# Expert outputs added through a second accumulator pair, spread over a column group; gates and scales fetched once for two experts

## The chip, the cores and the metric

The kernel runs on one core of a Trainium2 chip. Its engines run side by side and meet through semaphores: TensorE (PE; its weight loads are listed apart as PEld), VectorE (DVE), ScalarE (ACT), GpSimd (POOL) and SyncE (SP), which issues the weight transfers. Each engine takes its instructions in the order in which the program gives them. The metric is the device time of one execution in microseconds (us); the profile shows one execution, taken by the hardware profiler.

## The reference

Two decoder layers on 256 tokens of width 1024, in float32. Each layer has attention and a convolution that share an input and an output projection, and then a channel mixer: a dense SwiGLU in layer 0, routed experts in layer 1. The change touches the routed experts only. With `h` the normed tokens, they compute

```
logits = h @ router                       # 256 x 8
top_logit, top_e = top_k(logits, 2)       # two experts of each token
gate = softmax(top_logit)                 # one gate for each of the two
y_e = (silu(h_e @ wg[e]) * (h_e @ wu[e])) @ wd[e]     # h_e: the tokens that chose expert e
out = x + sum over the two experts of gate * y_e
```

with `wg`, `wu` of 1024 x 3584 and `wd` of 3584 x 1024 for each of eight experts.

## The kernel before

All weights stream from HBM through nine tiles of 1 MB (`raw`, line 165, issued by SP as a tile comes free). For float32 precision each matmul is made of three: a weight half tile is split by ACT into a rounded part `wh` (line 189) and by DVE into the rest `wl` (line 190), and `mm3` (lines 275 to 277) multiplies the high part by both and the low part by the high one. There are four pairs of `wh`/`wl` buffers, so splits run up to three half tiles ahead of PE.

The expert stage begins near 590 us and runs over the experts `e` (0 to 7), and in each over seven column groups `fc` of 512 hidden columns. `moe_in` (line 1308) makes the gate product in a bank of pool A and the up product in one of pool B (`pg`; eight steps `k` of three matmuls each), ACT applies SiLU, DVE multiplies (`sgm`, line 1329). `moe_out` (line 1347) adds the down product of the previous column group into `pd`, and in its middle `moe_tr` turns `sgm` by four transposes (`pt`, line 288) and splits it into `fh`, `fl`. The program is written out by hand in this order; nothing reorders it.

PSUM has eight banks: two of pool A, two of pool B, and two pairs of the pool `pacc` (`acc_bank`, line 97, a tile of two banks). `pd` of an expert takes one pair, so that consecutive experts alternate between the two pairs; the last expert takes the first bank of each. Small works are queued in the list `beside` and taken out one at a time behind the gate product's odd steps `k` (line 1322), four in a column group.

Which token sits in which of 128 slots of an expert is a one-hot matrix (`oh`, line 1229). Three things of an expert go through it:

- the tokens themselves, gathered by `gather` (line 1233) for a pair of experts in column groups 2 and 3 of the odd expert before;
- `turn_one_hot` (line 1378), behind the down product of column group 5: two transposes of the one-hot into a bank of pool A (`poh`), an ACT copy (`ohT`), then, in the same bank, two matmuls that fetch the expert's gate for each slot (`ge`, one column) with a DVE copy to `sgate`, and two that fetch the token scale of the next expert (`rs`, one column) with a DVE copy to `srs`;
- `combine` (line 1398): after an expert's last down product ACT and DVE make `yh` and `yl`, its output times the gates in two parts (`scaled`, lines 1394 and 1395). In column group 1 of the next expert four combines, for two column halves `n` and two token blocks `b`, multiply the turned one-hot by them into a bank of pool B (`pcomb`, lines 1402 and 1403) and DVE adds that to `xt` (line 1404). They stand in `beside`, so behind gate steps 1, 3, 5 and 7. The up product that follows needs a bank of the same pool B.

A last loop serves experts chosen by more than 128 tokens; it reads the gates and scales from the routing's own tiles.

Of the kernel before, what the change touches and what calls it, by code (L numbers as in the profile page):

```python
# [23 lines left out]
NB = 2  # L24
# [45 lines left out]
def trunk(ctx: ExitStack, tc: tile.TileContext, x, positions, attn_norm_g, ffn_norm_g, w_in, w_out,  # L70
# [28 lines left out]
    # ------------------------------------------------------------------ the stream of weights  # L99
# [49 lines left out]
    class Stream:  # L149
        """Weight tiles in the order of use: loads run RAW tiles ahead, the split into two  # L150
        float32r parts runs WB - 1 half tiles ahead."""
# [21 lines left out]
        def whole(self):  # L173
            """the next tile that is used as it is, and its number"""
            n = self.order[1].pop(0)
            return n, self.raws[n]
# [29 lines left out]
        def take_group(self, n):  # L206
            """n parts of one half tile each that are used more than once: no half tile beyond
            the buffers is split before their use"""
            return [self.take(WB - j) for j in range(n)]
# [9 lines left out]
    # ------------------------------------------------------------------ first loads  # L219
# [17 lines left out]
    # ------------------------------------------------------------------ constants  # L237
# [24 lines left out]
    # ------------------------------------------------------------------ helpers  # L262
    def rsqrt_mean(dst, ss, n):
        """dst = (ss / n + eps) ** -0.5"""
        w = ss.shape[-1]
        p = ss.shape[0]
        nc.vector.tensor_scalar(dst, ss, 1.0 / n, EPS, op0=ALU.mult, op1=ALU.add)
        nc.gpsimd.tensor_tensor(dst, dst, nhalf[:p, :w], op=ALU.pow)
# [15 lines left out]
    def transpose_split(src, hi, lo, bank):  # L284
        """src [128, 512] -> hi/lo [128, 4, 128]"""
        pt = bank("pt").rearrange("p (k t) -> p k t", k=4)
        for k in range(4):
            nc.tensor.transpose(pt[:, k], src[:, k * P:(k + 1) * P], ident)  # L288
        evac_split(hi, lo, pt)

    class Norm:
        """The transposed rms norm of xt, block by block, as hi/lo [128, 8, 256]; res: what is
        added to xt first"""
# [44 lines left out]
    def boundary(key, nrm, tails, heads, banks, **more):  # L338
        """the end of one part and the start of the next, with the norm between them; the order is
        that of the letters: o, a unit of the end (the last four those of the second token block);  # L340
        h, a unit of the start for the first block; z y x and a q u t, the norm of the two blocks;
        m, half a weight tile to split"""
        ops = dict(o=lambda: tails.pop(0)(), h=lambda: heads.pop(0)(), m=stream.more,
                   z=lambda: nrm.scale(0), y=lambda: nrm.mul(0), x=lambda: nrm.tr(0, banks),
                   a=lambda: nrm.add(1), q=lambda: nrm.square(1), u=lambda: nrm.mul(1), t=lambda: nrm.tr(1, banks),
                   **more)
        for c in BOUNDS[key]:
            ops[c]()

    # ------------------------------------------------------------------ rest of the setup  # L350
# [103 lines left out]
    def rope(sm, v, cs, sn):  # L454
        """v [n, heads, 64]; the first 16 of the last axis rotated in place"""
        n, h = v.shape[0], v.shape[1]
        t1 = sm.tile([P, HEADS, 16], F32, name="rope1", bufs=1)[:n, :h]
        t2 = sm.tile([P, HEADS, 16], F32, name="rope2", bufs=1)[:n, :h]
        csb = cs.rearrange("p a b -> p (a b)")[:, None, :].to_broadcast([n, h, 16])
        nc.vector.tensor_tensor(t1, v[:, :, :16], csb, op=ALU.mult)  # L460
        nc.vector.tensor_tensor(t2[:, :, :8], v[:, :, 8:16],
                                sn[:, 0][:, None, :].to_broadcast([n, h, 8]), op=ALU.mult)
        nc.vector.tensor_tensor(t2[:, :, 8:], v[:, :, :8],
                                sn[:, 1][:, None, :].to_broadcast([n, h, 8]), op=ALU.mult)
        nc.vector.tensor_tensor(v[:, :, :16], t1, t2, op=ALU.add)

    # ================================================================== layers
    for layer in range(DEPTH):
# [16 lines left out]
        # ---- queries, token-major  # L485
# [70 lines left out]
        # ---- inputs of the convolution, channel-major: two chunks of 128 channels at a time  # L556
# [28 lines left out]
        # causal depthwise conv, tap by tap beside other work: the first taps of a chunk on VectorE,  # L585
        # some on TensorE, the others multiplied on ScalarE and summed on GpSimd
# [20 lines left out]
        def tap_p(pair, j, first, last):  # L607
            """a tap of two chunks on TensorE, by diagonal matrices"""
# [32 lines left out]
        # ---- keys and values of the causal branches: token-major  # L641
# [41 lines left out]
        # ---- attention: the two causal branches, 512 score columns a step; the steps of both  # L683
        # token blocks form one pipeline
# [26 lines left out]
        # ---- inputs of the compressed branch and gates, channel-major  # L711
# [50 lines left out]
        # ---- compressed keys and values  # L762
# [74 lines left out]
        # ---- the steps of attention after the scores  # L837
# [79 lines left out]
        # ---- layer norm of the conv over channels and swish  # L917
# [52 lines left out]
        # ---- output projection  # L970
# [64 lines left out]
        # ---- channel mixer  # L1035
# [5 lines left out]
        # the scale of the tokens is left out where the experts apply it  # L1041
# [9 lines left out]
        def logits(b):  # L1051
            """the router's logits of a token block, channel-major"""
            bs = slice(b * P, (b + 1) * P)
            for k in range(DK):
                nc.tensor.matmul(pl[:16, bs], rt2[:, k], hT[:, k, bs], start=(k == 0), stop=False)
                nc.tensor.matmul(pl[:NE, bs], rt2[:, k, :NE], hTL[:, k, bs], start=False, stop=(k == DK - 1))
            nc.scalar.copy(lgT[:, bs], pl[:16, bs])
# [9 lines left out]
        if layer % 2 == 0:  # L1067
# [44 lines left out]
            def ffn_first():  # L1112
                """the first columns, token-major: the first token block starts before the second"""
# [70 lines left out]
        # ---- routed experts  # L1184
# [10 lines left out]
        # rank of each logit in its row; equal logits rank by index  # L1195
# [12 lines left out]
        # slot of each token within its expert: tokens before it that chose the same expert  # L1208
# [3 lines left out]
        ge = act.tile([P, NB, NE], F32, name="ge")  # L1212
# [20 lines left out]
        def gather(pair, banks):  # L1233
            """the tokens of a pair of experts, channel-major; in units of 256 channels and one part"""
# [23 lines left out]
        sgate = act.tile([P, NE], F32, name="sgate")  # L1258
        srs = act.tile([P, NE], F32, name="srs")
# [8 lines left out]
        def of_slots(dst, ps, e, src):  # L1268
            """a value of each token, for the tokens in the slots of an expert"""
            for b in range(NB):  # L1270
                nc.tensor.matmul(ps, ohs[e // 2].bitcast(F32)[:, b, e % 2], src[:, b:b + 1], start=(b == 0), stop=(b == NB - 1))
            nc.vector.tensor_copy(dst, ps)

        # experts chosen by more than 128 tokens: their number, indices, slots and gates
# [33 lines left out]
        def moe_in(e, fc, beside):  # L1308
# [4 lines left out]
            for bank in (bank_a, bank_b):  # L1313
                pg = bank("pg")
                for k in range(DK):
                    if first:
                        first.pop(0)()
                    if pgu and k == 2:
                        nc.scalar.activation(sg, pgu[0], AF.Silu, scale=srs[:, e:e + 1])
                    wh, wl = stream.take(2 if last and pgu else WB)  # L1320
                    mm3(pg, xg[:, k], xgL[:, k], wh, wl, k == 0, k == DK - 1)
                    if k % 2 and bank is bank_a and beside:
                        beside.pop(0)()
                if (e, fc) == (0, 0) and bank is bank_a:
                    of_slots(srs[:, 0:1], bank_b("psr")[:, :1], 0, rs)
                pgu.append(pg)
            for j in range(2 if last else 1):
                fs = slice(j * 256, (j + 1) * 256) if last else slice(0, 512)
                nc.vector.scalar_tensor_tensor(sg[:, fs], pgu[1][:, fs], srs[:, e:e + 1], sg[:, fs],
# [46 lines left out]
        ohTs, ys = {}, {}  # L1376

        def turn_one_hot(e):
            pt = bank_a("poh").rearrange("p (b t) -> p b t", b=4)
# [4 lines left out]
            of_slots(sgate[:, e:e + 1], pt[:, 2, :1], e, ge[:, :, e])  # L1384
            if e + 1 < NE:
                of_slots(srs[:, e + 1:e + 2], pt[:, 2, 1:2], e + 1, rs)

        def scaled(e, n):
            """the outputs of the expert times the gates, in two parts"""
# [4 lines left out]
            nc.scalar.activation(yh, pd, AF.Copy, scale=sgate[:, e:e + 1])  # L1394
            nc.vector.scalar_tensor_tensor(yl, pd, sgate[:, e:e + 1], yh.bitcast(F32),
                                           op0=ALU.mult, op1=ALU.subtract)

        def combine(e, n, b):
            ns = slice(n * 512, (n + 1) * 512)
            yh, yl = [y[:, ns] for y in ys[e]]  # L1400
            pc = bank_b("pcomb")
# [7 lines left out]
        beside = []  # L1409
        parts = [(n, b) for n in range(2) for b in range(NB)]  # L1410
        for e in range(NE):
            for fc in range(7):
                if fc == 1 and e:
                    beside += [lambda e=e, n=n, b=b: combine(e - 1, n, b) for n, b in parts]
# [3 lines left out]
                if fc == 2 and e % 2 == 1 and e + 1 < NE:  # L1418
                    beside += gather((e + 1) // 2, (bank_b, bank_b))
                if down_first(layer, NE - 1 - e, fc):  # L1420
# [10 lines left out]
                if fc == 5:  # L1431
                    turn_one_hot(e)
# [6 lines left out]
        # slots 128..255 of the experts that have them  # L1439
# [101 lines left out]
```

## Time and profile before

| | |
|---|---|
| median of three runs | 1623.56 us |
| the three runs | 1615.91, 1625.65, 1623.56 us |
| span of the profiled execution, first to last instruction | 1617.5 us |
| its own time, with what lies around the span | not recorded apart from the three runs |
| PE busy, whole span | 1546.0 us, 96% |
| DVE busy | 1342.1 us, 83% |
| ACT busy | 1093.4 us, 68% |
| DMA, mean rate | 268 GB/s over the span |
| TensorE clock granted, mean | 0.971 of full speed |

A matmul's record lasts longer than the distance to the next one, since matmuls overlap; how long a step takes is therefore read from the distance between starts. In the timeline an idle time of the engine before an instruction stands in brackets with what ended it. A clock of 0.50 is 1.2 GHz, of 1.00 it is 2.4 GHz.

### The profile page before, as it was taken

Reading aid. Unit: us, or ns where it says so; the run is one execution under the profiler, and the core shown is the slowest. Engines: PE = TensorE matmul, PEld = TensorE weight load, DVE = VectorE, ACT = ScalarE, POOL = GpSimd, SP = SyncE. Lnnn points to the kernel's source line nnn. Section 1 sums busy time; section 2 is a strip of 40 time slices with the busy share of each in tenths; the row PEclk is TensorE's granted clock in tenths of the full one; section 3 lists DMA queues with packets and bytes.
Section 4 is the critical chain, followed back from the end, with each engine's and each line's share of the span. In section 5 each row is a group of like instructions: output and inputs, shape, how many; then the busy total and the mean of one; then the engine's idle time right before and its main releaser. Section 6 shows DMA issues by size and latency. Waiting matters only on the chain.

```text
span 1617.5 us, 21390 instructions
## 1 busy us (share of the span) xinstructions
PE 1546.0 (96%) x7861; PEld 1294.0 (80%) x7861; DVE 1342.1 (83%) x1647; ACT 1093.4 (68%) x1430; POOL 126.0 (8%) x152
## 2 busy tenths in 40 slices
PE   6989999999997989999999999999999999999997
PEld 5977899999796768878877877887877877878785
DVE  7898655554789889989989989989989989998995
ACT  5765544444466568777877877777877777777774
POOL 2453000000155200000000000000000000000000
PEclk9978999999997999999999999999999999999998
DMA  9700585546632249999999998999999999998990
GB/s 307 223 27 1 187 304 182 183 167 198 158 105 79 79 151 373 378 323 335 362 336 337 371 337 314 359 349 338 371 339 330 338 353 329 367 369 314 362 364 27
DMA packets 197744, 433.75 MB, mean 268 GB/s; under 512 B 10346, under 2 KB 28978, under 8 KB 197636
## 3 DMA queue, kind: packets, MB, share of 16 engines
q1 hardware_dynamic: 196902, 432.02, 75.6%
q8 instruction: 63, 1.03, 0.3%
q0 software_dynamic: 288, 0.30, 0.1%
q14 instruction: 45, 0.37, 0.1%
q10 hardware_dynamic: 446, 0.03, 0.0%
HBM read 431.27 MB, written 1.05 MB: 267 GB/s over the span
## 4 chain that ended last, share of the span: by engine, by line
PE 77%; DVE 17%; ACT 3%; issue 2%; DMA 1%; POOL 0%; SPq 0%; DVEq 0%; ACTq 0%
PE pg L275 12%; PE pg L277 12%; PE pg L276 12%; PE pd L277 7%; PE pd L276 7%; PE pd L275 7%; DVE wl L190 5%; DVE cv L593 4%; PE pgu L275 3%; PE pgu L277 3%; PE pgu L276 3%; PE pt L288 2%; ACT wh L189 1%; PE pgx L1243 1%; DVE xt L1404 1%
## 5 line engine op out<-in xcount | busy, mean ns | idle before, releaser
L190 DVE TENSOR_TENSOR wl<-raw,wh 128x1024 fp32r<-128x1024 f32 x808 | 981.3, 1227 | 189.3 <-ACT wh L189 164.7
L189 ACT CAST wh<-raw 128x1024 fp32r<-128x1024 f32 x808 | 845.9, 1052 | 326.7 <-PE pg L277 126.4
L275 PE MATMUL pg<-wh,xgH 128*128 128x512 f32 x896 | 353.8, 395 | 6.5 <-DVE xt L1404 6.5
L277 PE MATMUL pg<-wh,xgL 128*128 128x512 f32 x896 | 353.5, 394 | 0.0
L276 PE MATMUL pg<-wl,xgH 128*128 128x512 f32 x896 | 352.5, 393 | 0.0
L275 PE MATMUL pd<-wh,fh 128*128 128x512 f32 x560 | 226.5, 404 | 0.1
L276 PE MATMUL pd<-wl,fh 128*128 128x512 f32 x560 | 222.2, 397 | 1.3 <-DVE wl L190 1.3
L277 PE MATMUL pd<-wh,fl 128*128 128x512 f32 x560 | 222.9, 398 | 0.0
L275 PEld LDWEIGHTS pg<-wh,xgH 128*128 128x128 f32 x896 | 170.3, 190 | 43.8 <-ACT wh L189 9.3
L277 PEld LDWEIGHTS pg<-wh,xgL 128*128 128x128 f32 x896 | 169.9, 190 | 36.5 <-DVE xgL L1247 0.5
L276 PEld LDWEIGHTS pg<-wl,xgH 128*128 128x128 f32 x896 | 170.5, 190 | 35.8 <-DVE wl L190 0.3
L276 PEld LDWEIGHTS pd<-wl,fh 128*128 128x128 f32 x560 | 105.8, 189 | 24.9 <-DVE wl L190 2.0
L277 PEld LDWEIGHTS pd<-wh,fl 128*128 128x128 f32 x560 | 105.6, 189 | 25.1 <-DVE fl L272 0.2
L275 PEld LDWEIGHTS pd<-wh,fh 128*128 128x128 f32 x560 | 105.9, 189 | 22.8 <-ACT fh L271 0.3
L275 PE MATMUL pgu<-hFH,wh 128*128 128x256 f32 x384 | 108.9, 284 | 0.8 <-DVE posT L452 0.8
L277 PE MATMUL pgu<-hFH,wl 128*128 128x256 f32 x384 | 108.7, 283 | 0.0
L276 PE MATMUL pgu<-hFL,wh 128*128 128x256 f32 x384 | 108.7, 283 | 0.0
L603 POOL TENSOR_TENSOR cvg<-cvg,tap 128x256 f32<-128x256 f32 x108 | 97.4, 929 | 75.4 <-ACT tap L602 71.9
L275 PEld LDWEIGHTS pgu<-hFH,wh 128*128 128x128 f32 x384 | 73.7, 192 | 1.1 <-PE pgk L1080 0.9
L276 PEld LDWEIGHTS pgu<-hFL,wh 128*128 128x128 f32 x384 | 73.7, 192 | 0.2
L277 PEld LDWEIGHTS pgu<-hFH,wl 128*128 128x128 f32 x384 | 73.7, 192 | 0.0
L593 DVE SCALAR_TENSOR_TENSOR cv<-hpad,cw,cv 128x256 f32<-128x256 f32 x124 | 72.2, 635 | 0.0
(371 smaller groups left out, 1655.1 us busy)
## 6 DMA issues: line engine op xcount, KB each, us to landing
raw<-in_moe_w_gate_dram SPq DMA_DIRECT2D x112, 1024.0 KB, 5.5
raw<-in_moe_w_up_dram SPq DMA_DIRECT2D x112, 1024.0 KB, 5.7
raw<-in_moe_w_down_dram SPq DMA_DIRECT2D x112, 1024.0 KB, 5.1
raw<-in_w_in_dram SPq DMA_DIRECT2D x18, 1024.0 KB, 9.5
raw<-in_ffn_w_gate_dram SPq DMA_DIRECT2D x14, 1024.0 KB, 7.9
raw<-in_ffn_w_up_dram SPq DMA_DIRECT2D x14, 1024.0 KB, 5.1
raw<-in_ffn_w_down_dram SPq DMA_DIRECT2D x14, 1024.0 KB, 4.9
raw<-in_w_out_dram SPq DMA_DIRECT2D x8, 1024.0 KB, 10.6
```

The lines of the kernel that those rows point to most:

```text
L189: nc.scalar.copy(h, r)
L190: nc.vector.tensor_tensor(lo, r, h.bitcast(F32), op=ALU.subtract)
L275: nc.tensor.matmul(dst, ah, bh, start=start, stop=False, skip_group_check=skip)
L276: nc.tensor.matmul(dst, ah, bl, start=False, stop=False, skip_group_check=skip)
L277: nc.tensor.matmul(dst, al, bh, start=False, stop=stop, skip_group_check=skip)
L288: nc.tensor.transpose(pt[:, k], src[:, k * P:(k + 1) * P], ident)
L593: nc.vector.scalar_tensor_tensor(cv[:, c], src, cw5[layer][:, c, j:j + 1], cv[:, c], op0=ALU.mult, op1=ALU.add)
L603: nc.gpsimd.tensor_tensor(cvg[:, c], cvg[:, c], tap, op=ALU.add)
L1243: nc.tensor.matmul(pgx, src[:, b, k * P:(k + 1) * P], ohs[pair][:, b].rearrange("p e s -> p (e s)"), start=(m == 0 and b == 0), stop=(m == ...
L1404: nc.vector.tensor_tensor(xt[:, b, ns], xt[:, b, ns], pc, op=ALU.add)
```

## The change

In column group 1 the four combines come from a list of their own, `spread`, taken out behind steps 1 and 5 of the gate product and of the up product. They write into an accumulator pair: `pcs[e]` is one `acc_bank` tile, and token block `b` uses its bank `b`. The last expert's combines keep pool B.

Token scales and gates of all experts sit in one tile `tv` (scale and eight gates for each token), for which DVE copies `rs` once in the routing. `slot_values` fetches all nine values for both experts of a pair by two units of two matmuls, in column group 4 of expert 0 and of each odd expert before the pair, and one DVE copy takes them to `sv`. Expert 0's first scale is still fetched alone at the beginning. `turn_one_hot` keeps its two transposes and the ACT copy, goes to `beside` in column group 5 (behind gate step 1), and uses pool B. Comments and docstrings are dropped elsewhere.

```
-        ge = act.tile([P, NB, NE], F32, name="ge")
+        tv = act.tile([P, NB, 1 + NE], F32, name="tv")
+        ge = tv[:, :, 1:]
+        nc.vector.tensor_copy(tv[:, :, 0], rs)
...
-        sgate = act.tile([P, NE], F32, name="sgate")
-        srs = act.tile([P, NE], F32, name="srs")
+        sv = act.tile([P, NE, 1 + NE], F32, name="sv")
+        srs = [sv[:, e, 0:1] for e in range(NE)]
+        sgate = [sv[:, e, 1 + e:2 + e] for e in range(NE)]
...
+        def slot_values(pair):
+            ps = {}
+            def unit(j):
+                if j == 0:
+                    ps["v"] = bank_b("psv")[:, :2 * (1 + NE)].rearrange("p (e n) -> p e n", e=2)
+                for b in range(NB):
+                    nc.tensor.matmul(ps["v"][:, j], ohs[pair].bitcast(F32)[:, b, j], tv[:, b],
+                                     start=(b == 0), stop=(b == NB - 1))
+                if j == 1:
+                    nc.vector.tensor_copy(sv[:, 2 * pair:2 * pair + 2], ps["v"])
+            return [lambda: unit(0), lambda: unit(1)]
...
                     if k % 2 and bank is bank_a and beside:
                         beside.pop(0)()
+                    if k % 4 == 1 and spread:
+                        spread.pop(0)()
...
         def turn_one_hot(e):
-            pt = bank_a("poh").rearrange("p (b t) -> p b t", b=4)
+            pt = bank_b("poh").rearrange("p (b t) -> p b t", b=4)
...
             nc.scalar.copy(ohTs[e], pt[:, :NB])
-            of_slots(sgate[:, e:e + 1], pt[:, 2, :1], e, ge[:, :, e])
-            if e + 1 < NE:
-                of_slots(srs[:, e + 1:e + 2], pt[:, 2, 1:2], e + 1, rs)
...
-            pc = bank_b("pcomb")
+            if e == NE - 1:
+                pc = bank_b("pcomb")
+            else:
+                if (n, b) == (0, 0):
+                    pcs[e] = acc_bank("pcomb")
+                pc = pcs[e][:, b]
...
                 if fc == 1 and e:
-                    beside += [lambda e=e, n=n, b=b: combine(e - 1, n, b) for n, b in parts]
+                    spread += [lambda e=e, n=n, b=b: combine(e - 1, n, b) for n, b in parts]
...
+                if fc == 4 and (e == 0 or e % 2 == 1 and e + 1 < NE):
+                    beside += slot_values((e + 1) // 2)
+                if fc == 5:
+                    beside += [lambda e=e: turn_one_hot(e)]
...
-                if fc == 5:
-                    turn_one_hot(e)
```

## Rows read from the trace of the kernel before

**Rows 1.** Busy time by stretch: us, PE, PEld, DVE, ACT, POOL, clock, DMA share, GB/s

```profile
720.00:845.00 125.00, 122.87 (x558) 100.19 (x557) 112.18 (x113) 95.01 (x105) 0.00 (x0) 0.99 0.93 337
...
902.80:919.70 16.90, 16.90 (x78) 13.85 (x76) 15.70 (x15) 13.55 (x15) 0.00 (x0) 1.00 1.01 367
```

**Rows 2.** Waits from 720 us on: who waited for whom, us, times, longest

```profile
ACT wh L189 <- PE pg L277: 110.1, 254, 3.0
...
PE pg L275 <- DVE xt L1404: 6.5, 7, 0.9
...
PE pd L276 <- DVE wl L190: 1.3, 2, 0.8
```

**Rows 3.** Timeline of PE at expert 1's turned one-hot: start, us, what

```profile
813.18 0.40 PE L277 MATMUL pd<-wh,fl 128*128 128x512 f32 x1
...
814.25 0.61 PE L1271 MATMUL poh<-ge,oh 128*128 128x1 f32 x4 [0.46 <-ACT ohT L1383]
815.18 0.60 PE L1271 MATMUL poh<-rs,oh 128*128 128x1 f32 x4 [0.32 <-DVE sgate L1272]
815.64 0.48 PE L275 MATMUL pg<-wh,xgH 128*128 128x512 f32 x1
...
816.19 0.63 PE L277 MATMUL pg<-wh,xgL 128*128 128x512 f32 x1
816.62 0.63 PE L275 MATMUL pg<-wh,xgH 128*128 128x512 f32 x1
```

**Rows 4.** Timeline of PE around four transposes inside a down product

```profile
809.93 0.40 PE L277 MATMUL pd<-wh,fl 128*128 128x512 f32 x1
...
810.52 0.48 PE L275 MATMUL pd<-wh,fh 128*128 128x512 f32 x1
```

**Rows 5.** Stretches of 3.41 us after a turned one-hot (two) and after a combine

```profile
816.17:819.58 3.41, 3.41 (x9) 2.64 (x8) 1.31 (x2) 1.04 (x1) 0.00 (x0) 0.50 0.78 229
...
687.00:690.41 3.41, 3.41 (x17) 2.78 (x16) 2.13 (x2) 1.78 (x2) 0.00 (x0) 1.00 0.68 209
...
730.06:733.47 3.41, 3.41 (x15) 2.85 (x16) 3.38 (x4) 1.74 (x3) 0.00 (x0) 1.00 0.84 294
```

**Rows 6.** Timeline of PE at the combines in column group 1 of expert 1

```profile
722.81 0.39 PE L275 MATMUL pg<-wh,xgH 128*128 128x512 f32 x1
...
725.82 0.39 PE L277 MATMUL pg<-wh,xgL 128*128 128x512 f32 x1
726.59 0.47 PE L1402 MATMUL pcomb<-yh,ohT 128*128 128x512 f32 x1 [0.39 <-DVE xt L1404]
...
728.74 0.40 PE L1403 MATMUL pcomb<-yl,ohT 128*128 128x512 f32 x1
730.06 0.47 PE L275 MATMUL pg<-wh,xgH 128*128 128x512 f32 x1 [0.92 <-DVE xt L1404]
```

**Rows 7.** Timeline of PE at the combines of expert 2

```profile
853.42 0.40 PE L275 MATMUL pg<-wh,xgH 128*128 128x512 f32 x1
...
856.70 0.47 PE L1402 MATMUL pcomb<-yh,ohT 128*128 128x512 f32 x1
```

**Rows 8.** Timeline of DVE in column group 1 of expert 1

```profile
725.76 0.68 DVE L1404 TENSOR_TENSOR xt<-xt,pcomb 128x512 f32<-128x512 f32 x1
726.36 1.22 DVE L190 TENSOR_TENSOR wl<-raw,wh 128x1024 fp32r<-128x1024 f32 x1
...
736.67 0.74 DVE L1329 SCALAR_TENSOR_TENSOR sgm<-pg,srs,sgm 128x512 f32<-128x512 f32 x1
```

**Rows 9.** Timeline of ACT: scaled outputs of expert 0 and of expert 7

```profile
722.46 0.69 ACT L1394 ACTIVATE yh<-pd,sgate 128x512 fp32r<-128x512 f32 x1 [0.92 <-DVE yl L1395]
...
1606.08 1.38 ACT L1394 ACTIVATE yh<-pd,sgate 128x512 fp32r<-128x512 f32 x2 [5.73 <-PE pd L277]
```

**Rows 10.** The page's DMA issues: count, KB each, us to landing

```profile
raw<-in_moe_w_gate_dram SPq DMA_DIRECT2D x112, 1024.0 KB, 5.5
```

**Rows 11.** Timeline of DVE in the routing

```profile
577.84 0.16 DVE L1214 TENSOR_REDUCE mx<-lg 128x2 f32<-128x16 f32 x1
```

More of the change, by code (lines that the diff above doesn't have):

```diff
@@ L1266, in gate_values, with slot_scale @@
             nc.vector.tensor_tensor(ge, ge, gs[:, :, None].to_broadcast([P, NB, NE]), op=ALU.mult)
-        def of_slots(dst, ps, e, src):
+        def slot_scale():
+            ps = bank_b("psr")[:, :1]
             for b in range(NB):
-                nc.tensor.matmul(ps, ohs[e // 2].bitcast(F32)[:, b, e % 2], src[:, b:b + 1], start=(b == 0), stop=(b == NB - 1))
-            nc.vector.tensor_copy(dst, ps)
+                nc.tensor.matmul(ps, ohs[0].bitcast(F32)[:, b, 0], rs[:, b:b + 1], start=(b == 0), stop=(b == NB - 1))
+            nc.vector.tensor_copy(srs[0], ps)
+        def slot_values(pair):
[9 more added lines that the diff above has]
+            return [lambda: unit(0), lambda: unit(1)]
         ov = act.tile([P, NE], F32, name="ov")
@@ L1318, in moe_in @@
                     if pgu and k == 2:
-                        nc.scalar.activation(sg, pgu[0], AF.Silu, scale=srs[:, e:e + 1])
+                        nc.scalar.activation(sg, pgu[0], AF.Silu, scale=srs[e])
                     wh, wl = stream.take(2 if last and pgu else WB)
@@ L1323, in moe_in @@
                         beside.pop(0)()
+                    if k % 4 == 1 and spread:
+                        spread.pop(0)()
                 if (e, fc) == (0, 0) and bank is bank_a:
-                    of_slots(srs[:, 0:1], bank_b("psr")[:, :1], 0, rs)
+                    slot_scale()
                 pgu.append(pg)
@@ L1328, in moe_in @@
                 fs = slice(j * 256, (j + 1) * 256) if last else slice(0, 512)
-                nc.vector.scalar_tensor_tensor(sg[:, fs], pgu[1][:, fs], srs[:, e:e + 1], sg[:, fs],
+                nc.vector.scalar_tensor_tensor(sg[:, fs], pgu[1][:, fs], srs[e], sg[:, fs],
                                                op0=ALU.mult, op1=ALU.mult)
@@ L1374, in moe_out @@
                     scaled(e, n)
-        ohTs, ys = {}, {}
+        ohTs, ys, pcs = {}, {}, {}
         def turn_one_hot(e):
-            pt = bank_a("poh").rearrange("p (b t) -> p b t", b=4)
+            pt = bank_b("poh").rearrange("p (b t) -> p b t", b=4)
             for b in range(NB):
@@ L1393, in scaled @@
             pd = pds[e][n] if e == NE - 1 else pds[e][:, n]
-            nc.scalar.activation(yh, pd, AF.Copy, scale=sgate[:, e:e + 1])
-            nc.vector.scalar_tensor_tensor(yl, pd, sgate[:, e:e + 1], yh.bitcast(F32),
+            nc.scalar.activation(yh, pd, AF.Copy, scale=sgate[e])
+            nc.vector.scalar_tensor_tensor(yl, pd, sgate[e], yh.bitcast(F32),
                                            op0=ALU.mult, op1=ALU.subtract)
@@ L1408, in trunk @@
         prev = None
-        beside = []
+        beside, spread = [], []
         parts = [(n, b) for n in range(2) for b in range(NB)]
```

## The prediction

> **What bounds the kernel now.** I read the busy time by stretch first, then the waits, then the timelines of single engines at the places that the change touches. Over a stretch of 125 us in the expert stage PE is busy 122.87 us and DVE 112.18 us; in an undisturbed column group PE fills all of the 16.90 us and DVE 15.70 us [rows 1]. The waits say the same from the other side: ACT waited 254 times, 110.1 us in all, for PE to free a buffer before it could split the next weights, while PE waited for a split of the down weights only twice, 1.3 us [rows 2]. So PE sets the pace here, and a stop of PE is paid in full unless another engine runs into PE's pace. Transfers are covered: a 1 MB tile lands 5.5 us after its issue [rows 10], a column group takes six of them in 16.90 us, 2.8 us each, and nine buffers therefore give some 25 us.
>
> One unit recurs below. From 722.81 to 725.82 us PE started 13 further matmuls [rows 6], so two neighbours stand 0.23 us apart at full clock.
>
> **The turned one-hot and the fetches.** Now each expert has a stop behind column group 5. From the last down matmul to the first gate matmul pass 815.64 - 813.18 = 2.46 us [rows 3], 2.23 us more than 0.23. Inside it PE waits for ACT's copy out of the bank, fetches gates, waits for the DVE copy, fetches scales. Experts 0 to 6 have this; expert 7 has no second fetch, 815.18 - 814.25 = 0.93 us less, so 1.30 us. Sum: 7 x 2.23 + 1.30 = 16.9 us.
>
> Afterwards two transposes stay for each expert. Four of them lengthen a distance from 0.23 to 0.59 us [rows 4], so two cost 0.18 us, eight times 1.4 us. A fetch unit is four short records again (two token blocks, two passes), and four such take 815.64 - 815.18 = 0.46 us [rows 3]. No row shows nine columns instead of one. Below, 0.46 us holds, since the records are as many; above, four full matmuls of 512 columns would take 4 x 0.23 = 0.92 us. Nine is near one, so I take 0.46, eight units, 3.7 us (up to 7.4). The part gains 16.9 - 1.4 - 3.7 = 11.8 us (8.1 at the other end).
>
> The ACT copy and the one DVE copy of a pair lie beside PE's next gate steps, because the up product that follows takes the other bank of pool B. If that cover failed, PE would wait 0.46 us for ACT as now [rows 3], 3.7 us in eight experts. The ACT copy waits for two transposes, and the casts queue behind it; DVE waits for these casts, and PE for DVE only after the three half tiles of lead, 18 x 0.23 = 4.1 us. I cost the wait at nothing. No DMA moves.
>
> **The clock.** After expert 1's one-hot the granted clock is 0.50 (1.2 GHz) for 3.41 us, with 9 matmuls, where a stretch after a combine has 15 at 1.00 [rows 5]. Two neighbours then stand 816.62 - 816.19 = 0.43 us apart [rows 3], so eight distances lose 0.20 us each, 1.6 us. Five of the eight experts show such a stretch right behind the one-hot (1, 2, 4, 5, 6); expert 0 does not [rows 5], nor do 3 and 7. Before each one PE had done little but short records for about 2.4 us. The stop of 1.09 us at a combine (below) is followed by full clock [rows 5], in all seven experts that have one. As the change leaves no stop much longer than that one, I take all five as gone: 8.0 us (bounds 0 and 8.0).
>
> **The combines.** In expert 1 the third combine begins 0.77 us behind its neighbour, and the up product 730.06 - 728.74 = 1.32 us behind the fourth, both waiting for a DVE add that must empty a bank of pool B [rows 6]. That loses 0.54 and 1.09 us. Experts 3 and 5 are alike; in 2, 4, 6 and 7, which build no new one-hots there, the third combine is hardly late (853.42 + 14 x 0.23 = 856.64 against 856.70 us [rows 7]) and the up product waits as long: seven such waits [rows 2]. Sum: 3 x 1.63 + 4 x 1.1 = 9.3 us.
>
> With the pair, the up product shares no bank with the combines, and that wait goes. What is late next is the second combine. The pair is one tile, and a pair seems to be held by one engine at a time: ACT's second `yh` of expert 0 waited 0.92 us for DVE's first `yl`, though they read different banks of one `pd` pair, while expert 7, whose `pd` are two tiles, runs both `yh` in 1.38 us without a break [rows 9]. Then the second combine, now behind gate step 5, waits for the first add. Its turn would be 722.81 + 12 x 0.23 = 725.57 us; the add ends at 725.76 + 0.68 = 726.44 [rows 8] and PE follows at 726.59, as the third combine does now [rows 6]: 1.02 us lost. In the even experts and in 7 it is 853.42 + 2.76 = 856.18 against 856.70 [rows 7], 0.52 us. The third comes 14 distances later, at 729.8 us; by then DVE has done two splits and the second add (726.36 + 2 x 1.2 + 0.68 = 729.4), so it does not wait, nor does the fourth. Behind the waiting combine are queued only the gate matmuls, priced with it. The product `sgm` is wanted 48 distances after the second combine, at 737.6 us; DVE, without a pause from 726.36 us on, ends it near 737.0 (now 736.67 + 0.74 [rows 8]). New stops: 3 x 1.02 + 4 x 0.52 = 5.1 us. Gain 9.3 - 5.1 = 4.2 us (7.4 at the other end, see the first rival).
>
> **The routing.** The copy of `rs` stands on DVE ahead of the reduction whose like took 0.16 us [rows 11], on the way to the first one-hots, with PE idle: 0.2 us lost (0 to 0.2).
>
> **Sum.** 11.8 + 8.0 + 4.2 - 0.2 = 23.8 us. On the profiled span that is 1617.5 to 1593.7. That execution's own time is not recorded beyond its span; the median, 1623.56, lies 6.1 us above it and one run, 1615.91, below it, so runs differ by some 10 us, which six half-clock stretches more or fewer would make (an estimate at 1.6 us each). I subtract from the median: 1599.8 us, as 1599.5.
>
> **First rival: no wait inside the pair.** If the program keeps engines apart by bank and not by tile, the second combine runs at 725.57 us. Then `sgm`, near 737.0, is late for its transposes at 725.57 + 48 x 0.23 = 736.6, some 0.6 us with the latency of 0.15, in experts 1, 3 and 5. The gain becomes 3 x 1.0 + 4 x 1.1 = 7.4 instead of 4.2: 1596.6 us. Against it stand the waits of `yh` [rows 9]. The Trainium skill speaks for it: its page "PSUM — Partial Sum Buffer" (section "PSUM bank collisions raise a hardware error") says that two engines may not touch one bank's quadrant at once and that accesses to different banks run clean. By that rule alone the time is 1596.6 us; the rows show a wait that it does not ask for. Chance 0.20.
>
> **Second rival: the drops of the clock stay**, caught by the stops and fetches that remain. Three of eight one-hots without a drop [rows 5] show that the stop alone does not decide. Gain 15.8 us: 1607.8. Chance 0.15.
>
> **Third rival, slower: the clock falls at the spread interruptions.** Eight turned one-hots, eight fetch units and 28 combines stand singly between gate and up matmuls. If each drew a half-clock stretch, 44 x 1.6 = 70 us would be added to the forecast: 1670 us. From 15 drops on (23.8 / 1.6) the kernel is slower than before, from 25 by over 1%. Against it: 28 combines are there already and none is followed by one [rows 5]. The Trainium skill knows such a case: "TensorE: Matmul & The Clock Gate", section "A second HAM failure mode: psum-queue depth-cycling", reports a kernel in which small idle times between groups of matmuls on changing PSUM banks made the clock go back and forth. The trace does not bear it out so far. Chance 0.08.
>
> **Fourth: the fetches and copies cost as much as they save**, PE waiting for ACT or DVE in column groups 4 and 5, where DVE has little room (15.70 of 16.90 us [rows 1]). Without the 11.8 us: 1611.6. Chance 0.07.
>
> **Numbers.** The forecast has 0.50. Its own range is 1595 to 1604 (3.7 us for dearer fetches, some 3 us if the median run had two drops more). Taking in the first and second rival and most of the fourth gives 1590 to 1611. A measurement can tell about 1% from no change, 16 us: faster means below 1607.3, slower above 1639.8. Faster: 0.50 + 0.20 + half of the second rival, 0.77. Slower: most of the third, 0.06. Same: the rest, 0.17.
>
> **What would show it.** Right: no `poh` fetch between column groups 5 and 6 and a gate matmul 0.23 us behind the last down matmul; no stretch at 0.50 in the expert stage before the last products; the up product of column group 1 no longer waiting for `xt`, and the second `pcomb` waiting 1.0 or 0.5 us for it. First rival: no such wait, and `pt` waiting for `sgm` in experts 1, 3 and 5. Wrong: half-clock stretches behind combines or fetches, PE waiting for `wl` or `wh`, or an expert's length falling by less than 1 us.

## The result and the profile after

The changed kernel takes 1595.55 us, the median of 4 runs (1593.36 to 1597.49), against 1624.29 us of the kernel before beside it (4 runs, 1615.91 to 1625.65): a ratio of 0.983, with a 95% interval of 0.981 to 0.986. 1599.5 us was forecast, with a range of 1590 to 1611. All medians of this document leave out one execution, of a kernel further below, which took 5051.78 us.

The profiled execution of after took 1595.13 us, close to its median. Its span is 1593.3 us, 24.2 us less than before's; 23.8 were forecast. The head of its page, with the clock in 40 slices:

```profile
span 1593.3 us, 21310 instructions
...
PE 1534.5 (96%) x7833; PEld 1289.9 (81%) x7833; DVE 1337.6 (84%) x1637; ACT 1093.3 (69%) x1430; POOL 122.1 (8%) x152
...
PEclk9978999999997789999999999999999999999999
```

From the sixteenth slice on (597 us), where the experts run, every slice shows the top digit. The same by stretches of after: the layers ahead with the experts' beginning, the expert stage, 125 us of it, then 3.41 us behind expert 0's turned one-hot and 3.41 us around the second combine (PE, PEld, DVE, ACT, POOL busy, clock, DMA share, GB/s):

```profile
0.00:588.00 588.00, 542.94 (x3349) 482.33 (x3350) 418.44 (x731) 315.26 (x596) 122.10 (x152) 0.92 0.47 153
...
588.40:1588.30 999.90, 991.16 (x4485) 807.31 (x4483) 918.77 (x907) 777.73 (x834) 0.00 (x0) 1.00 0.94 344
...
720.00:845.00 125.00, 124.17 (x572) 101.85 (x571) 114.89 (x117) 97.33 (x109) 0.00 (x0) 1.00 0.97 351
...
672.57:675.98 3.41, 3.41 (x18) 2.82 (x17) 2.76 (x3) 2.74 (x4) 0.00 (x0) 1.00 1.03 377
728.80:732.21 3.41, 3.41 (x16) 2.77 (x15) 3.41 (x5) 2.10 (x3) 0.00 (x0) 1.00 0.92 330
```

Where before PE was busy for 122.87 of 125 us [rows 1], it is now for 124.17 us, and it issues 572 matmuls there instead of 558. The stretch behind the one-hot holds 18 matmuls at full clock, against 9 at half clock before [rows 5].

The timeline of PE in after: expert 0's first scale, which is still fetched alone (`psr`, one column), a fetch unit, a turned one-hot, and the second combine in experts 1 and 2 (start, us, what; in brackets the idle time before and what ended it):

```profile
595.22 0.50 PE L1276 MATMUL psr<-rs,oh 128*128 128x1 f32 x4
595.58 0.47 PE L275 MATMUL pg<-wh,xgH 128*128 128x512 f32 x1
...
654.26 0.39 PE L277 MATMUL pg<-wh,xgL 128*128 128x512 f32 x1
654.50 0.51 PE L1287 MATMUL psv<-tv,oh 128*128 128x9 f32 x4
654.86 0.49 PE L275 MATMUL pg<-wh,xgH 128*128 128x512 f32 x1
655.18 0.40 PE L276 MATMUL pg<-wl,xgH 128*128 128x512 f32 x1
...
672.20 0.40 PE L277 MATMUL pg<-wh,xgL 128*128 128x512 f32 x1
672.43 0.38 PE L1403 MATMUL poh<-ident,oh 128*128 128x128 f32 x2
672.57 0.47 PE L275 MATMUL pg<-wh,xgH 128*128 128x512 f32 x1
672.89 0.39 PE L276 MATMUL pg<-wl,xgH 128*128 128x512 f32 x1
...
726.77 0.39 PE L277 MATMUL pg<-wh,xgL 128*128 128x512 f32 x1
727.95 0.50 PE L1426 MATMUL pcomb<-yh,ohT 128*128 128x512 f32 x1 [0.79 <-DVE xt L1428]
...
853.93 0.39 PE L277 MATMUL pg<-wh,xgL 128*128 128x512 f32 x1
854.59 0.50 PE L1426 MATMUL pcomb<-yh,ohT 128*128 128x512 f32 x1 [0.26 <-DVE xt L1428]
```

The fetch and the transposes stand between gate matmuls without a wait. What they cost is the distance that they add. A fetch unit adds 0.36 us, and the distance behind it is 0.32 instead of 0.23: 0.45 us in all, where 0.46 was taken. That 0.46 us was read from a fetch of one column behind a wait; `psr`, with no wait ahead of it, takes 595.58 - 595.22 = 0.36 us, as the nine columns do. Two transposes add 0.14 + 0.09 = 0.23 us, where 0.18 was taken. The second combine is late as forecast, by 727.95 - 726.77 - 0.23 = 0.95 us in expert 1 and by 0.43 us in expert 2.

The waits of after from 715 us on (in all, times, longest), to be read beside [rows 2]:

```profile
ACT wh L189 <- PE pg L277: 88.6, 235, 1.7
...
PE pcomb L1426 <- DVE xt L1428: 3.9, 8, 0.8
...
PE pd L276 <- DVE wl L190: 1.3, 2, 0.8
```

The wait of the up product for `xt` (6.5 us in 7 places before) is gone; the wait of the second combine has come in its place, in seven experts. (The eighth place, 0.42 us, is in the last expert, whose combines stay in pool B.) ACT still waits for PE as before: PE sets the pace.

### The profile page after: what moved, and what is told of

Its sections match the earlier page's. It is cut to its first block, busy times and chain, and to the rows that moved or that the text cites. A ratio compares the mean times of both kernels' runs of the same rounds, so it can differ in the third digit from the quotient of the medians.

```text
span 1593.3 us, 21310 instructions
## 1 busy us (share of the span) xinstructions
PE 1534.5 (96%) x7833; PEld 1289.9 (81%) x7833; DVE 1337.6 (84%) x1637; ACT 1093.3 (69%) x1430; POOL 122.1 (8%) x152
## 4 chain that ended last, share of the span: by engine, by line
PE 80%; DVE 14%; ACT 3%; issue 2%; DMA 1%; POOL 0%; SPq 0%; DVEq 0%; ACTq 0%
PE pg L275 12%; PE pg L277 12%; PE pg L276 12%; PE pd L277 8%; PE pd L276 8%; PE pd L275 7%; DVE cv L593 4%; DVE wl L190 4%; PE pgu L275 3%; PE pgu L277 3%; PE pgu L276 3%; PE pt L288 2%; ACT wh L189 1%; PE pgx L1246 1%; DVE nm L704 1%
## 5 line engine op out<-in xcount | busy, mean ns | idle before, releaser
L603 POOL TENSOR_TENSOR cvg<-cvg,tap 128x256 f32<-128x256 f32 x108 | 93.5, 891 | 80.1 <-ACT tap L602 76.3
```

What stands on the lines that cost most here:

```text
L603: nc.gpsimd.tensor_tensor(cvg[:, c], cvg[:, c], tap, op=ALU.add)
```

## The experiments

The theory behind the forecast was on record before these runs, in three parts: stops of PE are paid in full; a long one is paid a second time in half clock; and the second combine waits because the pair is one tile. The rivals were those of the prediction. Besides the time, the length of an expert is compared, from the first `yh` of the expert before to its own first `yh`, in one profiled execution each. Experts 3 and 4 stand for the odd ones (which build the next one-hots) and the even ones:

| us | time (median) | expert 3 | expert 4 |
|---|---|---|---|
| before | 1622 to 1624 | 129.03 | 126.19 (half clock) |
| combines alone | 1616.57 | 128.31 | 123.87 |
| fetches alone | 1602.27 | 127.85 | 122.45 |
| after | 1595.55, 1596.09 | 127.13 | 121.75 |
| one-hot in its old place | 1597.17 | 127.19 | 121.80 |
| old place and one fetch | 1603.40 | 128.23 | 122.73 |
| two tiles | 1592.18 | 126.34 | 121.19 |

**The combines alone.** The kernel before, with this part of the change only:

```
+                    if k % 4 == 1 and spread:
+                        spread.pop(0)()
...
-            pc = bank_b("pcomb")
+                if (n, b) == (0, 0):
+                    pcs[e] = acc_bank("pcomb")
+                pc = pcs[e][:, b]
...
-                    beside += [... combine(e - 1, n, b) ...]
+                    spread += [... combine(e - 1, n, b) ...]
```

> The kernel before with the combine part alone (spread list and accumulator pair); the turned one-hot and its fetches stay behind column group 5. My theory, that the two parts are separate terms: the stop of 2.2 us at each turned one-hot stays and with it half-clock stretches right behind four to six of the eight; the up product's wait of 1.09 us goes and the second combine waits 1.02 us (experts 1, 3, 5) or 0.52 us. The distance from one expert's first yh to the next falls by 0.6 us, seven times, so 4 us less than before, about 1620. Rival: the clock falls at the one-hot because of what the combines did earlier in the expert; then no stretch at 0.50 stands in the expert stage, and the time falls by 4 + 8 = 12 us, about 1612.

Measured 1616.57 us (6 runs, 1612.02 to 1618.38) against 1622.13, ratio 0.995 [0.994, 0.997]. Stretches of 3.41 us right behind the one-hots of experts 0 to 6 in this kernel (columns as above):

```profile
694.44:697.85 3.41, 3.41 (x9) 2.68 (x9) 1.50 (x2) 1.14 (x2) 0.00 (x0) 0.50 0.80 258
824.14:827.55 3.41, 3.41 (x9) 2.67 (x8) 1.69 (x2) 1.04 (x1) 0.00 (x0) 0.50 0.78 237
949.80:953.21 3.41, 3.41 (x17) 2.80 (x16) 1.95 (x3) 2.23 (x3) 0.00 (x0) 1.00 0.69 245
1078.10:1081.50 3.40, 3.40 (x17) 2.81 (x16) 1.98 (x3) 2.21 (x3) 0.00 (x0) 1.00 1.00 349
1201.90:1205.30 3.40, 3.40 (x16) 2.82 (x15) 1.98 (x3) 2.14 (x3) 0.00 (x0) 1.00 0.72 231
1329.32:1332.73 3.41, 3.41 (x10) 2.65 (x10) 1.29 (x2) 0.70 (x1) 0.00 (x0) 0.50 0.73 231
1455.61:1459.02 3.41, 3.41 (x9) 2.65 (x9) 1.66 (x2) 1.04 (x1) 0.00 (x0) 0.50 0.75 232
```

Half clock follows the one-hots of experts 0, 1, 5 and 6 here; before it was 1, 2, 4, 5 and 6. So the one-hot's stop brings it without the old combines too, though not every time. Expert 3, at full clock in both, is 0.72 us shorter, expert 1, at half clock in both, 0.68 us (0.61 forecast for odd experts). The time fell by more than 4 us; which half-clock stretches a run has differs, so this part's 4 to 5 us is read from the experts' lengths.

**The fetches and the turned one-hot alone.** After, with the combines as they were:

```
-                    pcs[e] = acc_bank("pcomb")
-                pc = pcs[e][:, b]
+            pc = bank_b("pcomb")
...
-                    spread += [... combine(e - 1, n, b) ...]
+                    beside += [... combine(e - 1, n, b) ...]
```

> The kernel after with the combines as before (behind gate steps 1, 3, 5, 7, in pool B); only the fetches and the turned one-hot are changed. My theory: the stops behind column group 5 go (11.8 us) and all half-clock stretches with them (8.0 us), less 0.2 us in the routing; the combines keep 7 waits of 1.09 us and three of 0.54 us. About 19.6 us less than before, 1604. Rival: the stops at the combines also feed the drops of the clock, so that stretches at 0.50 remain behind some experts' combines or fetches: 11.6 us less, 1612.6.

Measured 1602.27 us (1597.48 to 1604.10), ratio 0.987 [0.985, 0.989]: 19.9 us less than before beside it, 19.6 expected. The expert stage of this kernel and two of its waits between 700 and 1590 us, each view in a fence of its own:

```profile
592.20:1599.10 1006.90, 992.37 (x4486) 807.05 (x4485) 921.95 (x907) 779.76 (x834) 0.00 (x0) 1.00 0.94 341
```

```profile
PE pg L275 <- DVE xt L1423: 6.4, 7, 0.9
...
PE pcomb L1421 <- DVE xt L1423: 1.1, 3, 0.4
```

The clock is full throughout, and the up product's wait is the old one. All the clock's gain behind the one-hots therefore lies in this part, and the rival by which the half clock stays falls.

**The turned one-hot in its old place.** After, with only the fetches away from it:

```
-            pt = bank_b("poh")...
+            pt = bank_a("poh")...
...
-                if fc == 5:
-                    beside += [lambda e=e: turn_one_hot(e)]
...
+                if fc == 5:
+                    turn_one_hot(e)
```

> The kernel after, with the two transposes and the ACT copy of the one-hot moved back to their old place behind the down product of column group 5, in pool A; the fetches stay out of it. My theory: the stop came from the two fetches that waited in the same bank for ACT and DVE, not from the place; the gate product that follows takes the other bank of pool A, so there is no stop and no half-clock stretch, and the time is that of the kernel after within 1.5 us. Rival: the place itself, between down and gate product, makes PE wait (0.5 us or more for ACT, eight times) or lets the clock fall: 4 to 12 us more than the kernel after.

Measured 1597.17 us (1595.86 to 1599.47), ratio 0.985 [0.983, 0.987]. PE in this kernel, between the last down matmul and the first gate matmul:

```profile
688.73 0.40 PE L277 MATMUL pd<-wh,fl 128*128 128x512 f32 x1
688.97 0.38 PE L1403 MATMUL poh<-ident,oh 128*128 128x128 f32 x2
689.10 0.47 PE L275 MATMUL pg<-wh,xgH 128*128 128x512 f32 x1
```

PE does not stop: the gate product goes to the other bank of pool A. The stop came from the fetches in the one-hot's bank, not from the place of the transposes; moving them gives nothing measurable.

**One fetch again.** The kernel of the last experiment, with one gate fetch again in the one-hot's bank and a DVE copy behind it. The fetched value goes to a tile that nothing reads; the rest is computed as in after.

```
             nc.scalar.copy(ohTs[e], pt[:, :NB])
+            for b in range(NB):
+                nc.tensor.matmul(pt[:, 2, :1], ohs[e // 2]..., ge[:, b, e:e + 1], ...)
+            nc.vector.tensor_copy(sagain[:, e:e + 1], pt[:, 2, :1])
```

> The kernel with the transposes of the one-hot in their old place behind column group 5, and one fetch of the gates put back there in the same bank, with its DVE copy to a tile that nothing reads; the scales are not fetched there. That is about half of the stop of before: PE waits for ACT's copy, fetches, and goes on, 1.3 us in place of 2.2. My theory: it costs the stop alone, eight times 1.1 us more than without, 9 us, about 1605, and the clock stays at full speed as it did at expert 7 of the kernel before, whose stop was 1.3 us. Rival: half the stop is enough for the clock to fall behind several one-hots: 1.6 us more for each stretch, 1610 or more.

Measured 1603.40 us (1601.77 to 1605.65), ratio 0.987 [0.985, 0.990]. PE behind column group 5 of expert 0 in this kernel, and then its expert stage:

```profile
689.49 0.39 PE L277 MATMUL pd<-wh,fl 128*128 128x512 f32 x1
689.71 0.38 PE L1405 MATMUL poh<-ident,oh 128*128 128x128 f32 x2
690.56 0.61 PE L1409 MATMUL poh<-tv,oh 128*128 128x1 f32 x4 [0.46 <-ACT ohT L1407]
691.02 0.48 PE L275 MATMUL pg<-wh,xgH 128*128 128x512 f32 x1
```

```profile
590.10:1600.40 1010.30, 995.85 (x4517) 811.63 (x4515) 920.50 (x915) 777.34 (x834) 0.00 (x0) 1.00 0.94 340
```

The stop is back with 691.02 - 689.49 - 0.23 = 1.30 us, and an expert is 0.93 to 1.04 us longer (experts 4 and 3) than in the last experiment, where 1.1 was expected; the medians differ by 6.2 us, less than the 9 expected. The clock stays full. The eight stops of 1.3 us are paid once. The one of 2.23 us [rows 3], which experts 0 to 6 have, was paid twice in five of the seven before, and in four of the seven with the combines alone; each count is from one profiled execution.

**Two tiles for the combines.** After, with a tile of its own for each token block:

```
-                if (n, b) == (0, 0):
-                    pcs[e] = acc_bank("pcomb")
-                pc = pcs[e][:, b]
+                if n == 0:
+                    pcs[e, b] = acc_bank("pcomb")[:, 0]
+                pc = pcs[e, b]
```

> The kernel after, with the two token blocks of a combine in two accumulator tiles (the first bank of each) in place of two banks of one tile. My theory, that the program keeps engines apart by tile: the second combine no longer waits for xt (now 0.95 and 0.43 us of PE in the seven experts, 4.6 us in all); in experts 1, 3 and 5 the four transposes pt then wait some 0.5 us for sgm, as DVE has no slack there; 2 to 4 us less than the kernel after, about 1592.5. Rival 1: the wait is not the tile's but DVE's or the semaphore order's; the second combine still waits 0.4 to 1.0 us and the time is that of the kernel after. Rival 2: DVE gives all of it back, in waits for wl or sgm of the same sum: time as after within 1 us, but no wait for xt.

Measured 1591.25 us (four executions, 1590.68 to 1593.24; 1591.77 with the one of 5051.78), ratio 0.981 [0.979, 0.983]. The one left out was the profiled one, so the waits are read from the same kernel once more:

> The kernel with two accumulator tiles for the two token blocks once more, for a profile at the usual clock. Its runs gave 1591.8 us, some 4 us less than the kernel after. My theory, that the program keeps engines apart by tile: no pcomb waits for xt in the seven experts (4.6 us now), and pt waits about 0.5 us for sgm in experts 1, 3 and 5. Rival 1: the wait for xt is still there and the 4 us come from fewer half-clock stretches ahead of the expert stage. Rival 2: no wait for xt, but PE waits for wl instead, in sum less than 1 us better.

Measured 1592.18 us (1589.90 to 1593.38), ratio 0.980 [0.978, 0.982]. PE at the second combine of expert 1 in this kernel, and one of its waits from 700 us on:

```profile
729.19 0.39 PE L277 MATMUL pg<-wh,xgL 128*128 128x512 f32 x1
729.42 0.39 PE L1426 MATMUL pcomb<-yh,ohT 128*128 128x512 f32 x1
```

```profile
PEld pt L288 <- DVE sgm L1351: 1.3, 3, 0.4
```

The second combine follows its neighbour by 0.23 us. So the wait in after was due to the pair being one tile, and what is late next is what the first rival named: `sgm`, in the three odd experts, 0.4 us each at most. Odd experts gain 0.79 us over after, even ones 0.56.

**Three ways to be rid of both waits.** The pair kept, the second combine later (behind gate steps 1 and 7, up steps 3 and 7), and the next one-hots built in column group 0:

```
-                    if k % 4 == 1 and spread:
+                    if spread and k in ((1, 7) if bank is bank_a else (3, 7)):
...
-                if fc == 1 and e % 2 == 1 and e + 1 < NE:
+                if fc == 0 and e % 2 == 1 and e + 1 < NE:
                     one_hot(e + 1)
```

> The kernel after with two moves: the combines behind gate steps 1 and 7 and up steps 3 and 7 (now 1, 5, 1, 5), and the one-hots of the next pair built in column group 0 (now 1). One tile of two banks as in the kernel after. My theory: the second combine comes 1.4 us later, when the first add is done, so the 0.95 and 0.43 us of waiting go (4.6 us in all); DVE ends sgm 0.2 us late for its transposes in each of seven experts (1.4 us back): 3 us less than the kernel after, 1592.5. Rival: DVE is the limit in this column group, and PE waits 0.4 us or more for sgm in every expert: 0 to 1.5 us less than the kernel after.

Measured 1590.36 us (1589.31 to 1591.39), ratio 0.980 [0.978, 0.982], 2 us under the 1592.5 expected. The second combine does not wait, nor does `pt` wait for `sgm` in that column group, where 1.4 us was expected in all; one new wait is left, in the last expert:

```profile
PE pd L275 <- DVE xt L1428: 1.1, 1, 1.1
```

Two tiles and the one-hots in column group 0 (both edits as shown):

> Two accumulator tiles for the combines, and the one-hots of the next pair built in column group 0. My theory: neither a wait for xt (4.6 us now) nor for sgm, as the 0.86 us of one-hots leave DVE's crowded column group: 4 to 5 us less than the kernel after, 1591, and about 1 us less than the two tiles alone. Rival: the one-hots were not what made sgm late, and the time is that of the two tiles alone within 0.5 us, with the same waits.

Measured 1590.60 us (1587.75 to 1592.66), ratio 0.979 [0.977, 0.981]. Its odd experts take 126.1 us, 0.25 less than with two tiles alone: the `sgm` wait is gone.

The same, with the combines behind gate steps 3 and 5 and up steps 1 and 5 (`k in ((3, 5) if bank is bank_a else (1, 5))`):

> Two accumulator tiles, one-hots in column group 0, and the combines behind gate steps 3 and 5 and up steps 1 and 5, so that the first one comes after DVE has made yl. Theory: the wait of the first combine's second matmul for yl goes, 0.3 us in seven experts, 2 us less than with the two tiles and the early one-hots alone: about 1588.5, and 7 us less than the kernel after. Rival: ACT and DVE make yh and yl later than the first combine is wanted even then, or the third combine now waits for the first add; 1590.5 as without this move.

Measured 1590.09 us (1588.10 to 1591.23), ratio 0.980 [0.978, 0.981], where 1588.5 was expected. One of its waits from 700 us on:

```profile
PEld pt L288 <- DVE sgm L1351: 2.1, 6, 0.4
```

The first combine no longer waits for `yl`, but `sgm` is late again, in six places; an expert gains only 0.2 us. The three are the fastest versions, about 5.5 us under after, and alike within their runs.

**After once more**, on the same chip as the last one:

> The kernel after once more, beside the next one on the same chip and against more runs of the kernel before. Theory: about 1595.5 us, 28 us less than before; its runs lie closer together than those of before, as no half-clock stretch is left in the expert stage to come or go. Rival: the 28 us of the first four runs were 4 to 5 us of luck in the layers ahead of the experts, and the time is 1599.

Measured 1596.09 us (5 runs, 1593.07 to 1597.42), ratio 0.982 [0.981, 0.984]. The gain stands. That its runs would lie closer together than before's was not borne out: 4.35 us between fastest and slowest against 4.88 us.

## Why the prediction was right

**The ledger of the two profiled executions.** The first `yh` of expert 0 starts at 720.85 us before and at 722.30 after (1.4 us later), that of expert 7 at 1606.08 and 1582.01. So the seven experts between give 885.23 - 859.71 = 25.5 us, the stage ahead takes 1.4 back, and the tail gives 0.1: 24.2. The 25.5 us split by the run with the fetches alone, in which the same seven take 864.66 us. The lines for expert 0 before, for experts 0 and 7 after, and for the same two with the fetches alone (expert 7 before is in [rows 9]):

```profile
720.85 0.69 ACT L1394 ACTIVATE yh<-pd,sgate 128x512 fp32r<-128x512 f32 x1 [0.35 <-PE pd L277]
...
722.30 0.69 ACT L1413 ACTIVATE yh<-pd,sv 128x512 fp32r<-128x512 f32 x1 [0.35 <-PE pd L277]
1582.01 0.69 ACT L1413 ACTIVATE yh<-pd,sv 128x512 fp32r<-128x512 f32 x1 [4.17 <-PE pd L277]
...
726.48 0.69 ACT L1413 ACTIVATE yh<-pd,sv 128x512 fp32r<-128x512 f32 x1 [0.34 <-PE pd L277]
1591.14 1.39 ACT L1413 ACTIVATE yh<-pd,sv 128x512 fp32r<-128x512 f32 x2 [4.17 <-PE pd L277]
```

- **Fetches, one-hot and clock**: 885.23 - 864.66 = 20.6 us. Experts 1 and 3 of before do the same work, one followed by a half-clock stretch and the other not: 130.61 - 129.03 = 1.58 us (1.6 forecast). There were five in the steps forecast (8.0 us) and a sixth, below. Taken off at 1.6 us each, 11.0 us stay for fetches and one-hots in seven experts; the forecast's terms give 11.8 - (2.23 - 0.18 - 0.92) = 10.7 for these seven. The nine columns cost what one did: the lower bound was the right one.
- **The sixth stretch** was not forecast. Before has 3.41 us at half clock in expert 7's last products; PE in it (columns as above):

```profile
1601.24:1604.65 3.41, 3.41 (x9) 2.64 (x9) 0.81 (x1) 0.00 (x0) 0.00 (x0) 0.50 0.00 0
```

After has none ahead of 1588.3 us, by when its expert 7 is done with them. No step of the change touches that place. Just ahead of it PE waits 0.58 us for `sgm` and 0.77 and 0.50 us for `wl`; the row `pd` <- `wl` (1.3 us, 2 times) is the same in all eleven profiles, and the ten others have no half clock there. The combines alone, at the same place:

```profile
1601.34:1604.75 3.41, 3.41 (x16) 2.74 (x16) 0.80 (x1) 0.13 (x1) 0.00 (x0) 1.00 0.00 0
```

So this stretch most likely came with the execution and did not go by the change; what decides it is open. Expert 7 gains 3.37 us where the forecast's terms make 1.70, and the rest, 1.67 us, is luck of the profile.
- **Combines**: 864.66 - 859.71 = 4.95 us, 0.69 to 0.72 in each expert, where 4.2 was forecast. The waits measured 0.95 and 0.43 us, a little under 1.02 and 0.52. That they come from the tile and not from the bank is what the two-tile runs show. The Trainium skill's rule on banks ("PSUM — Partial Sum Buffer", section "PSUM bank collisions raise a hardware error") asks for no wait between two banks, and with two tiles the trace agrees with it. The first rival, without the wait, was put 2.9 us under the forecast; two tiles took 1592.18 us, 3.4 us under after (4.4 us by the lengths of the seven experts, 859.71 - 855.27).
- **The rivals.** The slower one, half clock at the spread interruptions, is refuted: 44 interruptions, and the clock is 1.00 from 588.4 to 1588.3 us. That the fetches cost as much as they save is refuted by 1602.27 us with them alone.
- **Luck.** That the profiles' 24.2 us stand so near to 23.8 is luck in part. The seven experts give 25.5 us where the forecast's terms make 10.7 + 8.0 + 4.2 = 22.9; the sixth stretch and the combines are most of the difference. The stage ahead took 1.4 us where the terms make a gain of 1.13 - 0.2 = 0.9.

**What was mis-sized is the base.** The sum was subtracted from the median of before, though its durations came from a faster execution. In the 25 later runs of before the span was 1621.4 us in the median (1617.7 to 1625.2), and the times lay some 2.2 us above the spans; the profiled one had 1617.5. Of the 6.1 us that the prediction saw between the median and the profiled span, some 2.2 us therefore lie around the span, and 3.9 are a faster execution.

Most of these 3.9 us seem to lie ahead of the seven experts. In seven of the eleven profiles PE has the same work up to the first `yh` of expert 0: after, twice, the fetches alone, the two tiles, and the three last versions (in which DVE builds two one-hots shortly before it). They reach it between 720.74 and 726.48 us, at 723.52 in the median. Before has the stop of 2.23 us besides, and still reaches it at 720.85. By the forecast's terms it would be 723.52 + 0.9 = 724.4, 3.6 us later, an estimate. Up to 575 us the granted clock is 0.95 in before's profile; in the ten other profiles it is 0.93 or 0.94. The seven experts of after, in contrast, took 859.71 and 859.66 us in its two profiles.

The mean clock points the same way: 0.971 in before's profile and 0.966 in the median of the 25 runs. After's nine runs have 0.972 in the median and its profiled one 0.971, so there the profile is typical. That makes the gain 28.7 us by the medians where the profiles give 24.2. Where the timed runs of before had their further half clock was not seen, since they leave only a mean.

## What to carry to other kernels

Price a stop of the engine that sets the pace by the distance between the matmuls around it, and look right behind it for a stretch of lower clock, which here made a stop of 2.2 us cost 3.8; with the stop down to 1.3 us the second price did not appear. Give two engines that meet in a PSUM pair two tiles, not one: the pair as one tile made PE wait 0.4 to 1.0 us for a bank that nobody was using, and the place of the interruptions can then be chosen by what the next engine has to deliver. Before subtracting a sum from a median, compare the profiled execution's span and mean clock with those of the timed runs.

## What the runs showed of the hardware

- Half clock behind the same stop is not fixed: experts 1, 2, 4, 5 and 6 in one kernel and 0, 1, 5 and 6 in another, at the same instructions. It can be put into a sum only by its share of the stops of 2.2 us, 5 of 7 and 4 of 7; of ten stops of 1.3 us (eight in the kernel with one fetch again, and expert 7 in before and with the combines alone) none had it. In one of eleven profiles it also came behind three waits of 0.50 to 0.77 us within 5 us.
- A fetch of nine columns took as long as one of one column: 0.36 us for four records of 128x9 and for four of 128x1, up to the start of the next full matmul and with no wait ahead. Behind a wait of PE, four of 128x1 took 0.46 us.
- The same work of PE up to the first `yh` of expert 0 ended up to 5.7 us apart in seven profiled executions (720.74 to 726.48); the seven experts behind that point took the same time within 0.05 us in the two profiles of after.
